# Sums of the FFN weights made in DRAM by accumulating GpSimd transfers, and eleven gated pairs by seven products

## The chip, the core and the metric

One core of a Trainium2 chip runs the whole program. The metric is the device time of one execution in microseconds; lower is better. The engines are TensorE (PE, matmuls), VectorE (DVE), ScalarE (ACT), GpSimd (POOL) and SyncE (SP, which here only issues transfers). Each engine works through its own instructions in a fixed order and waits on semaphores for the others.

## The reference, cut

One hybrid decoder layer over 16 meta tokens and 512 positions (528 columns), model width 1024, in float32:

```
u    = rmsnorm(h);  proj = u @ w_in                       # 52 column blocks of 128
a    = hgrn2(q, f, i, g)                                  # 8 heads, gated linear recurrence
b    = mamba2(z, xbc, dt)                                 # 16 heads, conv + SSD scan
h    = h + concat(a, b) @ w_out
n    = rmsnorm(h);  u = conv3(n @ w_up)                   # w_up: 1024 x 5632
gate, val = split(u)                                      # 22 blocks of 128 each
h    = h + (silu(gate) * val) @ w_down
y    = rmsnorm(h)[:, 16:]
```

## The kernel before

Features lie on the 128 partitions and tokens on the free axis. Every float32 weight tile (128x1024, 512 KB, called a chunk) is split into two `fp32r` parts, `hi` (an ACT copy) and `lo` (a DVE subtraction of `hi` from the raw tile), and every product is made of three matmuls: hi·hi, hi·lo and lo·hi. The list `chunks` holds all chunks in the order of use. `ahead` loads and splits two chunks further than the one in use; the tags `raw`, `whi` and `wlo` have three buffers each, so a chunk's raw load waits until the split three chunks earlier has been done, and its split waits until the matmuls three chunks earlier have been done. A list scheduler lays down each engine's order when the program is built, from priorities (weights are preferred by 100000, evacuations of PSUM by 150000).

The stages, in order of time: Mamba-2, then the eight HGRN heads (`hgrn_head`, three weight chunks each), `hgrn_norm` after heads 3 and 7, the eight gate products, the output projection, the FFN's up-projection, and the down-projection. `hgrn_norm` writes the inverse norms to DRAM (`rs_d`), reads each back spread over the partitions (`rb`) and multiplies each head's output `o` by it in place.

The up-projection works on 22 pairs of a gate block j and a value block 22+j. `KINDS` gives each pair a kind. U and N pairs are direct: two chunks, 96 matmuls of 258 or 256 columns (U uses tokens that are not yet normalised and scales the result). A W pair (`scheme`) halves the contraction and the tokens, in the manner of Strassen and Winograd, and makes seven half-size products instead of eight: 84 matmuls of 258 columns. Its weights come as three chunks from `scheme_weights`: `w0` is the gate block itself, `w2` holds the sums s1 and s2, and `w1` holds two further tiles plus a fourth sum s4 in buffers of the tag `ab`. Before, the two raw blocks are loaded (two transfers), and DVE makes four sums of 128x512 in SBUF. After the seven products, one ACT copy and six DVE additions (lines 965 to 971) put the results together out of PSUM, and `taps` applies the three-tap convolution.

`STEPS` and `SPLITS` hang other work on the pairs' ends: normalising the tokens, and splitting finished activations `ac` for the down-projection. POOL does a few memsets early on and four multiplications at the very end; it issues no transfer.

Of the kernel before, what the change touches and what calls it, by code (L numbers as in the profile page):

```python
# [7 lines left out]
F32 = mybir.dt.float32  # L8
# [3 lines left out]
ALU = mybir.AluOpType  # L12
# [3 lines left out]
P = 128  # L16
# [3 lines left out]
T0 = META - 2  # L20
NB = 4
DM = 1024
KD = DM // P
FF = 2816
KF = FF // P
# [22 lines left out]

KINDS = "UUUUUUUUNWNWWNWNWWNWWN"
STEPS = {0: (0, 1), 1: (2,), 2: (3,), 3: (4,), 4: (5,), 5: (6,), 6: (7,)}
SPLITS = {7: (0,), 8: (1, 2), 10: (3,), 13: (4,), 15: (5,), 18: (6,), 20: (7, 8), 21: range(9, 22)}
HT = 258
NUNSC = 5

# [4 lines left out]
def tile_block(ctx: ExitStack, tc: tile.TileContext, xT, w_in, w_dt, w_out, w_up, w_down,  # L61
               par, consts, consti, out, dbg=None):
    nc = tc.nc
    V, A, G, PE = nc.vector, nc.scalar, nc.gpsimd, nc.tensor

    cp = ctx.enter_context(tc.tile_pool(name="cp", bufs=1))
# [5 lines left out]
    dp = ctx.enter_context(tc.tile_pool(name="dp", bufs=1, space=DRAM))  # L72

    def slot(name, n=NT, dtype=F32, parts=P, tag="m"):
        return gp.tile([parts, n], dtype, tag=tag, name=name, bufs=TAGS[tag])

    def first(offset=100000):
        return tc.high_priority(offset=offset)
# [31 lines left out]
    V.memset(eps, EPS)  # L110
    LOGS = "natural_log_exp_and_others"
    warm = cp.tile([P, 1], F32, name="warm")
    with first(300000):
        w = A.activation(warm[:], eps[:], AF.Copy)
        with tc.issue_after(w.ins):
            A.preload_act_table_set(LOGS)
# [30 lines left out]
    chunks = [(("in", j), w_in[j], KD) for j in order]  # L147
# [3 lines left out]
    chunks += [(("out", j, s), w_out[j][:, s * KD * P:(s + 1) * KD * P], KD) for j, s in oorder]  # L151
    for j in range(KF):
        if KINDS[j] == "W":
            chunks += [(("w0", j), w_up[j], KD), (("w2", j), w_up[KF + j], KD), (("w1", j), None, KD)]
        else:
            chunks += [(("up", j), w_up[j], KD), (("up", KF + j), w_up[KF + j], KD)]
    def dn(j, k0, kc):
# [5 lines left out]
    wdone = {}  # L163
    wnext = [0]

    def raw_tile(key):
        return wp.tile([P, KD * P], F32, tag="raw", name="raw_" + "_".join(map(str, key)), bufs=3)

    def split_tiles(key):
        name = "_".join(map(str, key))  # L170
        return (wp.tile([P, KD * P], F32R, tag="whi", name=f"whi_{name}"),
                wp.tile([P, KD * P], F32R, tag="wlo", name=f"wlo_{name}"))
# [4 lines left out]
    def split_weights(raw, hi, lo, d, eng):  # L177
        A.activation(hi[:, d], raw[:, d], AF.Copy)  # L178
        eng.tensor_tensor(lo[:, d], raw[:, d], hi[:, d].bitcast(F32), ALU.subtract)  # L179

    HK = KD * P // 2
    sums = {}

    def split_half(x, hi, lo):
        A.activation(hi, x, AF.Copy)
        V.tensor_tensor(lo, x, hi.bitcast(F32), ALU.subtract)

    def scheme_weights(key, src):


        kind, j = key
        if kind == "w0":
            sums[j] = [raw_tile(key)]
            nc.sync.dma_start(sums[j][0][:], src)
            hi, lo = split_tiles(key)
            split_weights(sums[j][0], hi, lo, slice(0, 2 * HK), V)
            return hi, lo
        if kind == "w2":
            rg, rv = sums[j][0], raw_tile(key)
            nc.sync.dma_start(rv[:], src)  # L200
            s1, s2 = slot(f"s1_{j}", 512, tag="ab"), slot(f"s2_{j}", 512, tag="ab")
            V.tensor_tensor(s1[:], rv[:, 0:HK], rv[:, HK:], ALU.add)
            V.tensor_tensor(s2[:], s1[:], rg[:, 0:HK], ALU.add)
            sums[j] += [rv, s2]
            hi, lo = split_tiles(key)
            split_half(s1[:], hi[:, 0:HK], lo[:, 0:HK])
            split_half(s2[:], hi[:, HK:], lo[:, HK:])
            return hi, lo
        rg, rv, s2 = sums.pop(j)
        V.tensor_tensor(rv[:, 0:HK], rv[:, 0:HK], rg[:, 0:HK], ALU.add)  # L210
        V.tensor_tensor(rg[:, HK:], rg[:, HK:], s2[:], ALU.add)
        hi, lo = split_tiles(key)
        split_weights(rv, hi, lo, slice(0, 2 * HK), V)
        h4, l4 = slot(f"s4h_{j}", 512, F32R, tag="ab"), slot(f"s4l_{j}", 512, F32R, tag="ab")
        split_half(rg[:, HK:], h4[:], l4[:])
        return hi, lo, h4, l4

    def ahead(n):
        while wnext[0] < min(n, len(chunks)):
            key, src, kc = chunks[wnext[0]]  # L220
            if key[0] in ("w0", "w1", "w2"):
                with first():
                    wdone[key] = scheme_weights(key, src)
                wnext[0] += 1
                continue
            with first():
                raw, hi, lo = raw_tiles(key)
                d = slice(0, kc * P)
                nc.sync.dma_start(raw[:, d], src)
                split_weights(raw, hi, lo, d, V)  # L230
            wdone[key] = (hi, lo)
            wnext[0] += 1
# [24 lines left out]
    with first(200000):  # L257
        for k in range(0, KD, 2):
            d = slice(k * P, (k + 2) * P)
            for j, w, kx in ((BT, starts[0], k), (CT, starts[1], k + 1)):  # L260
                t = slot(f"x{kx}", tag="y")
# [8 lines left out]
        for k in range(KD):  # L270
# [3 lines left out]
            tag = "b0" if k < 4 else "b1"  # L274
            hi, lo = slot(f"v{k}_hi", dtype=F32R, tag=tag), slot(f"v{k}_lo", dtype=F32R, tag=tag)
# [23 lines left out]
    with first():  # L299
        for n, (a0, a1) in enumerate(((0, HALF), (HALF, NT))):  # L300
            p = bank(f"psn{n}")
# [49 lines left out]
    for n, (a0, a1) in enumerate(((0, HALF), (HALF, NT))):  # L351
        p = bank(f"psd{n}")[0:66, :]
# [305 lines left out]
    os_ = []  # L658
# [138 lines left out]

    for h in range(NH):
        hgrn_head(h)
        if h % 4 == 3:  # L800
            hgrn_norm(h - 3)
    oah, oal = [], []
    for h in range(NH):
# [6 lines left out]
        hi, lo = slot(f"oa{h}_hi", dtype=F32R), slot(f"oa{h}_lo", dtype=F32R)  # L810
# [10 lines left out]
    for j, s in oorder:  # L821
        w = weights("out", j, s)
# [10 lines left out]
        hi, lo = slot(f"u2h{j}", dtype=F32R, tag="u"), slot(f"u2l{j}", dtype=F32R, tag="u")  # L833
# [92 lines left out]
    def scheme(j):  # L926

        p1, p2, p6 = (bank(f"p{n}_{j}")[:, 0:HT] for n in (1, 2, 6))
        p75, p43 = banks2(f"p75_{j}"), banks2(f"p43_{j}")
        H = KD // 2  # L930
        b11 = [(nh[k][:, tails[0]], nl[k][:, tails[0]]) for k in range(H)]
        b21 = [(nh[k][:, tails[0]], nl[k][:, tails[0]]) for k in range(H, KD)]
        b22 = [(nh[k][:, tails[1]], nl[k][:, tails[1]]) for k in range(H, KD)]
        t1, t2, t3, t4 = ([t[n] for t in ts] for n in range(4))

        def mul(ps, hi, lo, xs):
            for k, (xh, xl) in enumerate(xs):
                wh, wl = hi[:, k * P:(k + 1) * P], lo[:, k * P:(k + 1) * P]
                PE.matmul(ps, wh, xh, start=k == 0, stop=False)  # L939
                PE.matmul(ps, wh, xl, start=False, stop=False)  # L940
                PE.matmul(ps, wl, xh, start=False, stop=k == H - 1)  # L941


        sg, sv, su = (slot(f"s{n}{j}", 2 * HT, tag=t) for n, t in (("g", "L"), ("v", "L"), ("u", "pr")))
        cs = [slot(f"fc{i}", 512, tag="pr") for i in (j, KF + j)]
        A_, B_ = slice(0, HT), slice(HT, 2 * HT)

        def two(ps):
            return ps[:].rearrange("p (a t) -> p a t", a=2)[:, :, 0:HT]

        def by_halves(t):
            return t[:].rearrange("p (a t) -> p a t", a=2)

        hi, lo = weights("w0", j)
        mul(p1, hi[:, 0:HK], lo[:, 0:HK], b11)
        mul(p2, hi[:, HK:], lo[:, HK:], b21)
        hi, lo = weights("w2", j)
        mul(p6, hi[:, HK:], lo[:, HK:], t2)
        mul(p75[:, 512:512 + HT], hi[:, 0:HK], lo[:, 0:HK], t1)
        hi, lo, h4, l4 = weights("w1", j)  # L960
        mul(p75[:, 0:HT], hi[:, 0:HK], lo[:, 0:HK], t3)
        mul(p43[:, 512:512 + HT], h4, l4, b22)
        mul(p43[:, 0:HT], hi[:, HK:], lo[:, HK:], t4)
        with evac():
            A.activation(sg[:, A_], p1, AF.Copy)
            V.tensor_tensor(sv[:, A_], sg[:, A_], p6, ALU.add)
            V.tensor_tensor(sg[:, A_], sg[:, A_], p2, ALU.add)
            V.tensor_tensor(by_halves(su), sv[:, A_].unsqueeze(1).broadcast_to([P, 2, HT]), two(p75), ALU.add)
            V.tensor_tensor(sv[:, B_], su[:, A_], p75[:, 512:512 + HT], ALU.add)
            V.tensor_tensor(sv[:, A_], su[:, A_], p43[:, 0:HT], ALU.add)  # L970
            V.tensor_tensor(sg[:, B_], su[:, B_], p43[:, 512:512 + HT], ALU.add)
        for c, r, i in ((cs[0], sg, j), (cs[1], sv, KF + j)):
            w = taps_of(j) if r is sg else [ntap[:, n * KF + j:n * KF + j + 1] for n in range(3)]
            taps(by_halves(c), by_halves(r), i, w, col(C_FB + i))
        return cs
# [157 lines left out]
```

## Time and profile before

| | us |
|---|---|
| median of 3 runs | 882.2 (881.79 to 883.04) |
| profiled execution, first to last instruction (span) | 880.9 |
| PE busy in it | 861.5 |
| DVE busy | 596.4 |
| ACT busy | 438.7 |
| POOL busy | 8.9 |

The profile gives its execution's own time only as the span, 880.9 us; what lies around the span is not in it, and the median of the runs is 1.3 us above the span. "Busy" counts the union of an engine's instructions; a matmul is pipelined, so one of 258 columns is shown with some 282 ns although the next begins after 120 ns. In a table by stretches, "busy (x n)" is the busy time and the number of instructions in the stretch. In a timeline, the brackets hold the idle time before an instruction and what ended it.

### The profile page before, as it was taken

Reading aid. Unit: us, or ns where it says so; the run is one execution under the profiler, and the core shown is the slowest. Engines: PE = TensorE matmul, PEld = TensorE weight load, DVE = VectorE, ACT = ScalarE, POOL = GpSimd, SP = SyncE. Lnnn points to the kernel's source line nnn. Section 1 sums busy time; section 2 is a strip of 40 time slices with the busy share of each in tenths; the row PEclk is TensorE's granted clock in tenths of the full one; section 3 lists DMA queues with packets and bytes.
Section 4 is the critical chain, followed back from the end, with each engine's and each line's share of the span. In section 5 each row is a group of like instructions: output and inputs, shape, how many; then the busy total and the mean of one; then the engine's idle time right before and its main releaser. Section 6 shows DMA issues by size and latency. Waiting matters only on the chain.

```text
span 880.9 us, 16283 instructions
## 1 busy us (share of the span) xinstructions
PE 861.5 (98%) x6840; PEld 821.5 (93%) x6840; DVE 596.4 (68%) x1012; ACT 438.7 (50%) x688; POOL 8.9 (1%) x30
## 2 busy tenths in 40 slices
PE   7999999999999999999999999999999999999995
PEld 6999898999999999999999999999999999888885
DVE  6984977788776766444334469888999997633333
ACT  7638985966446444363222265445455555433221
POOL 1000000000000000000000000000000000000001
PEclk9999999999999999999999999999999999999998
DMA  7234242212221222245233223322133314243312
GB/s 247 91 114 154 88 133 72 73 53 69 73 62 60 100 70 72 85 137 163 97 96 97 89 81 96 97 96 90 56 117 100 120 56 131 66 110 105 90 43 95
DMA packets 29081, 84.64 MB, mean 96 GB/s; under 512 B 3128, under 2 KB 6712, under 8 KB 29008
## 3 DMA queue, kind: packets, MB, share of 16 engines
q1 hardware_dynamic: 26480, 80.02, 29.2%
q10 hardware_dynamic: 2528, 3.60, 1.4%
q8 instruction: 53, 0.87, 0.4%
q14 instruction: 20, 0.16, 0.1%
HBM read 81.45 MB, written 2.15 MB: 95 GB/s over the span
## 4 chain that ended last, share of the span: by engine, by line
PE 96%; ACT 1%; DMA 1%; DVE 1%; issue 1%; DVEq 0%; SPq 0%; ACTq 0%
PE pj L250 33%; PE pup L250 18%; PE pout L250 10%; PE pdn L1006 3%; PE pdn L1007 3%; PE pdn L1005 3%; PE p L939 3%; PE p L940 3%; PE p L941 3%; PE pdn L1019 1%; PE pdn L1021 1%; PE pdn L1020 1%; PE psy L550 1%; DMA x<-in_xT_dram 1%; PE psy L553 1%; PE pa L752 1%
## 5 line engine op out<-in xcount | busy, mean ns | idle before, releaser
L250 PE MATMUL pj<-u_lo,whi_in 128*128 128x272 f32 (+1 forms) x752 | 157.1, 288 | 0.0
L250 PE MATMUL pj<-u_hi,wlo_in 128*128 128x272 f32 (+1 forms) x752 | 156.3, 286 | 0.0
L250 PE MATMUL pj<-u_hi,whi_in 128*128 128x272 f32 (+1 forms) x752 | 155.3, 287 | 0.0
L250 PEld LDWEIGHTS pj<-u_lo,whi_in 128*128 128x128 f32 x752 | 116.2, 188 | 2.4 <-issue 1.9
L250 PEld LDWEIGHTS pj<-u_hi,wlo_in 128*128 128x128 f32 x752 | 116.6, 189 | 2.0 <-issue 1.9
L250 PEld LDWEIGHTS pj<-u_hi,whi_in 128*128 128x128 f32 x752 | 115.6, 188 | 2.4 <-issue 2.3
L179 DVE TENSOR_TENSOR wlo_in<-raw_in,whi_in 128x1024 fp32r<-128x1024 f32 (+1 forms) x58 | 64.3, 1108 | 55.6 <-ACT whi_in L178 55.4
L178 ACT ACTIVATE whi_in<-raw_in 128x1024 fp32r<-128x1024 f32 (+1 forms) x58 | 56.0, 966 | 64.0 <-PE pj L250 59.1
L179 DVE TENSOR_TENSOR wlo_dn<-raw_dn,whi_dn 128x1024 fp32r<-128x1024 f32 (+1 forms) x24 | 27.3, 1136 | 54.6 <-ACT whi_dn L178 54.6
L178 ACT ACTIVATE whi_dn<-raw_dn 128x1024 fp32r<-128x1024 f32 (+1 forms) x24 | 23.6, 987 | 73.8 <-PE pdn L1006 53.4
L1006 PE MATMUL pdn<-ac_lo,whi_dn 128*128 128x512 f32 (+1 forms) x154 | 55.9, 363 | 0.0
L1005 PE MATMUL pdn<-ac_hi,whi_dn 128*128 128x512 f32 (+1 forms) x154 | 55.6, 361 | 0.0
L1007 PE MATMUL pdn<-ac_hi,wlo_dn 128*128 128x512 f32 (+1 forms) x154 | 55.6, 361 | 0.0
L178 ACT ACTIVATE whi_up<-raw_up 128x1024 fp32r<-128x1024 f32 x28 | 29.7, 1060 | 46.8 <-PE pup L250 23.9
L250 PE MATMUL pup<-u2h,wlo_up 128*128 128x258 f32 (+1 forms) x256 | 51.6, 283 | 0.0
L250 PE MATMUL pup<-u2l,whi_up 128*128 128x258 f32 (+1 forms) x256 | 51.1, 281 | 0.0
L250 PE MATMUL pup<-u2h,whi_up 128*128 128x258 f32 (+1 forms) x256 | 51.1, 282 | 0.0
L178 ACT ACTIVATE whi_out<-raw_out 128x1024 fp32r<-128x1024 f32 x16 | 17.0, 1061 | 55.7 <-PE pout L250 29.9
L179 DVE TENSOR_TENSOR wlo_up<-raw_up,whi_up 128x1024 fp32r<-128x1024 f32 x28 | 34.2, 1220 | 9.8 <-ACT whi_up L178 9.7
L179 DVE TENSOR_TENSOR wlo_out<-raw_out,whi_out 128x1024 fp32r<-128x1024 f32 x16 | 19.6, 1225 | 30.1 <-ACT whi_out L178 30.1
L250 PEld LDWEIGHTS pup<-u2h,wlo_up 128*128 128x128 f32 x256 | 39.3, 188 | 0.1
L250 PEld LDWEIGHTS pup<-u2l,whi_up 128*128 128x128 f32 x256 | 39.3, 189 | 0.0
(357 smaller groups left out, 2186.4 us busy)
## 6 DMA issues: line engine op xcount, KB each, us to landing
raw_in<-in_w_in_dram SPq DMA_DIRECT2D x50, 512.0 KB, 3.6
raw_up<-in_w_up_dram SPq DMA_DIRECT2D x28, 512.0 KB, 3.6
raw_out<-in_w_out_dram SPq DMA_DIRECT2D x16, 512.0 KB, 3.6
raw_w<-in_w_up_dram SPq DMA_DIRECT2D x16, 512.0 KB, 3.7
raw_dn<-in_w_down_dram SPq DMA_DIRECT2D x16, 512.0 KB, 3.9
ab<-acum_d SPq DMA_DIRECT2D x16, 264.0 KB, 4.2
raw_dn<-in_w_down_dram SPq DMA_DIRECT2D x8, 384.0 KB, 3.1
rb<-rs_d SPq DMA_DIRECT2D x8, 257.0 KB, 4.3
```

The source lines that it names most:

```text
L178: A.activation(hi[:, d], raw[:, d], AF.Copy)
L179: eng.tensor_tensor(lo[:, d], raw[:, d], hi[:, d].bitcast(F32), ALU.subtract)
L250: PE.matmul(ps[:, O + a0:O + a1], w, x[:, a0:a1], start=s, stop=e)
L550: PE.matmul(psy[q0:q0 + 64, a0 - META:a1 - META], xdt[b][:, hc], Ls[h][:, a0:a1], start=True, stop=False)
L553: PE.matmul(psy[q0:q0 + 64, a0 - META:a1 - META], ss[b - 1][:, hc], abs_[h][:, a0:a1], start=False, stop=True)
L752: PE.matmul(pa[:, c:c + P], kA[:, META + c:META + c + P], qA[:, c:c + P], start=True, stop=True)
L939: PE.matmul(ps, wh, xh, start=k == 0, stop=False)
L940: PE.matmul(ps, wh, xl, start=False, stop=False)
L941: PE.matmul(ps, wl, xh, start=False, stop=k == H - 1)
L1005: PE.matmul(ps, wh, xh, start=k0 + k == 0, stop=False)
L1006: PE.matmul(ps, wh, xl, start=False, stop=False)
L1007: PE.matmul(ps, wl, xh, start=False, stop=k0 + k == KF - 1)
```

## The change

Eleven pairs instead of eight are of kind W; N pairs go from six to three. The four weight sums of a W pair are no longer made by DVE. Instead, `weight_sums` makes them in a DRAM tile `sums{j}` of four 128x512 slots by six GpSimd transfers per pair: two plain copies (512 KB each) lay down the first halves of the gate and the value block in slots 0 and 1 and the whole gate block in slots 2 and 3; then come accumulating transfers of 512, 256, 256 and 256 KB, each of which adds a further half block, or slot 0 itself, to slots already there. `scheme_weights` then loads ready sums: `w2` in one transfer, `w1` in three.

```
-KINDS = "UUUUUUUUNWNWWNWNWWNWWN"
+KINDS = "UUUUUUUUNWWWWNWWWWWWWN"
+WS = [j for j in range(KF) if KINDS[j] == "W"]
...
+    def weight_sums(js, behind):
+        gate = G.tensor_copy(tick[:], behind)
...
+        with tc.issue_after(gate.ins):
+            for j in js:
+                G.dma_start(ds[j][:, 0:2], halves[j][:, :, 0:HK])
+                G.dma_start(ds[j][:, 2:4], w_up[j].rearrange("p (n c) -> p n c", n=2))
+            for j in js:
+                G.dma_start(ds[j][:, 0:2], twice(w_up[KF + j][:, HK:]), accum_op=ALU.add)
+                G.dma_start(ds[j][:, 2], w_up[KF + j][:, 0:HK], accum_op=ALU.add)
+            for j in js:
+                G.dma_start(ds[j][:, 0], w_up[KF + j][:, 0:HK], accum_op=ALU.add)
+            for j in js:
+                G.dma_start(ds[j][:, 3], ds[j][:, 0], accum_op=ALU.add)
...
+        elif kind == "w2":
+            nc.sync.dma_start(raw[:], sumd[j][:, 0:2 * HK])
+        else:
+            s4 = slot(f"s4_{j}", 512, tag="ab")
+            nc.sync.dma_start(raw[:, 0:HK], sumd[j][:, 2 * HK:3 * HK])
+            nc.sync.dma_start(raw[:, HK:], w_up[KF + j][:, HK:])
+            nc.sync.dma_start(s4[:], sumd[j][:, 3 * HK:])
+        split_weights(raw, hi, lo, slice(0, 2 * HK), V)
...
-            V.tensor_tensor(s1[:], rv[:, 0:HK], rv[:, HK:], ALU.add)
-            V.tensor_tensor(s2[:], s1[:], rg[:, 0:HK], ALU.add)
...
-        V.tensor_tensor(rv[:, 0:HK], rv[:, 0:HK], rg[:, 0:HK], ALU.add)
-        V.tensor_tensor(rg[:, HK:], rg[:, HK:], s2[:], ALU.add)
...
     for h in range(NH):
         hgrn_head(h)
+        if h < len(WS) // 2 + len(WS) % 2:
+            weight_sums(WS[2 * h:2 * h + 2], os_[h][:, T0:T0 + 1])
```

The sums of two pairs hang on each of heads 0 to 5 (one pair on head 5): a POOL copy of one column of the head's output `o` into `tick` stands ahead of that head's twelve transfers. So POOL's queue now reads the `o` tiles that `hgrn_norm` later overwrites.

POOL, in the HGRN heads: before, nothing stands there. Now the queue between the copies into `tick` for heads 2 and 3 holds twelve transfers, of which the last eight and the copy for head 3 read as follows (`sums14` and `sums15` are the DRAM tiles of pairs 14 and 15, `o3` the output of head 3).

```order
L208 DMA sums14_3049<-in_w_up_dram 128x2x512
L209 DMA sums14_3049<-in_w_up_dram 128x512
L208 DMA sums15_3050<-in_w_up_dram 128x2x512
L209 DMA sums15_3050<-in_w_up_dram 128x512
L211 DMA sums14_3049<-in_w_up_dram 128x512
L211 DMA sums15_3050<-in_w_up_dram 128x512
L213 DMA sums14_3049<-sums14_3049 128x512
L213 DMA sums15_3050<-sums15_3050 128x512
L192 COPY tick_81<-o3_3326 128x1
```

The copy for head 3 stands behind all transfers of pairs 14 and 15, and each of these rows waits in the queue until the transfer it adds to has landed: L208 and L209 for the plain copies, L211 for L208, L213 for L211.

DVE, first norm of the HGRN heads (after head 3): before, the four in-place products on `o0` to `o3` stand together, ahead of work of head 4 (`mt0`, `S4`, `sc0`).

```order
L796 SCALAR_TENSOR_TENSOR o0_2482<-o0_2482,pt_75,rb0_3306 128x514
L796 SCALAR_TENSOR_TENSOR o1_2748<-o1_2748,pt_75,rb1_3310 128x514
L796 SCALAR_TENSOR_TENSOR o2_3014<-o2_3014,pt_75,rb2_3314 128x514
L796 SCALAR_TENSOR_TENSOR o3_3280<-o3_3280,pt_75,rb3_3318 128x514
L179 TENSOR_TENSOR wlo_in_14_3647<-raw_in_14_3645,whi_in_14_3646 128x1024
L757 COPY_PREDICATED mt0_2194<-maskA_77,pm4_3529 16x2
L666 TENSOR_SCALAR f5_3642<-f5_3642,lbt_480 128x528
L744 SCALAR_TENSOR_TENSOR S4_3545<-S4_3545,d128_4_3513,pS4_3544 128x128
```

Now:

```order
L814 SCALAR_TENSOR_TENSOR o0_2483<-o0_2483,pt_75,rb0_3367 128x514
L814 SCALAR_TENSOR_TENSOR o1_2764<-o1_2764,pt_75,rb1_3371 128x514
L181 TENSOR_TENSOR wlo_in_14_3723<-raw_in_14_3721,whi_in_14_3722 128x1024
L814 SCALAR_TENSOR_TENSOR o2_3045<-o2_3045,pt_75,rb2_3375 128x514
L775 COPY_PREDICATED mt0_2195<-maskA_77,pm4_3590 16x2
L684 TENSOR_SCALAR f5_3718<-f5_3718,lbt_481 128x528
L762 SCALAR_TENSOR_TENSOR S4_3606<-S4_3606,d128_4_3574,pS4_3605 128x128
L814 SCALAR_TENSOR_TENSOR o3_3326<-o3_3326,pt_75,rb3_3379 128x514
L777 COPY_PREDICATED sc0_2193<-maskA_77,pa4_3615 128x512
```

The product on `o3` moved behind the `mt0` copy and ahead of the `sc0` copy. Each of the products on `o0` to `o5` now also waits for POOL's copy out of that `o`.

PE, end of a run of W pairs before an N pair: before, pair 17 ended (`p43_17`), then four matmuls of the next W pair, 19, stood ahead of the N pair 18 (`pup18`); the same stood between pairs 9 and 10, and two matmuls of the down-projection between pairs 20 and 21.

```order
L941 MATMUL p43_17_8210<-t4_3_6874,wlo_w1_17_8219 128x258
L939 MATMUL p1_19_8469<-n0_hi_6009,whi_w0_19_8340 128x258
L940 MATMUL p1_19_8469<-n0_lo_6010,whi_w0_19_8340 128x258
L939 MATMUL p2_19_8470<-n4_hi_6015,whi_w0_19_8340 128x258
L940 MATMUL p2_19_8470<-n4_lo_6016,whi_w0_19_8340 128x258
L250 MATMUL pup18_8344<-n0_hi_6009,whi_up_18_8251 128x258
```

Now such a place stands between pairs 12 and 13:

```order
L961 MATMUL p43_12_7632<-t4_3_6958,wlo_w1_12_7640 128x258
L959 MATMUL p1_14_7888<-n0_hi_6093,whi_w0_14_7764 128x258
L960 MATMUL p1_14_7888<-n0_lo_6094,whi_w0_14_7764 128x258
L959 MATMUL p2_14_7889<-n4_hi_6099,whi_w0_14_7764 128x258
L960 MATMUL p2_14_7889<-n4_lo_6100,whi_w0_14_7764 128x258
L268 MATMUL pup13_7769<-n0_hi_6093,whi_up_13_7676 128x258
```

The two matmuls of the down-projection between pairs 20 and 21 stand as before; inside the runs 9 to 12 and 14 to 20 the W pairs follow each other directly.

More of the change, by code (lines that the diff above doesn't have):

```diff
@@ L112, in tile_block @@
     warm = cp.tile([P, 1], F32, name="warm")
+    tick = cp.tile([P, 1], F32, name="tick")
     with first(300000):
@@ L153, in tile_block @@
         if KINDS[j] == "W":
-            chunks += [(("w0", j), w_up[j], KD), (("w2", j), w_up[KF + j], KD), (("w1", j), None, KD)]
+            chunks += [((w, j), None, KD) for w in ("w0", "w2", "w1")]
         else:
@@ L181, in tile_block @@
     HK = KD * P // 2
-    sums = {}
+    sumd = {}
     def split_half(x, hi, lo):
@@ L186, in split_half, with twice @@
         V.tensor_tensor(lo, x, hi.bitcast(F32), ALU.subtract)
-    def scheme_weights(key, src):
+    def weight_sums(js, behind):
+        gate = G.tensor_copy(tick[:], behind)
+        halves = w_up.rearrange("(a j) p c -> j p a c", a=2)
+        ds = {}
+        for j in js:
+            t = dp.tile([P, 4 * HK], F32, name=f"sums{j}")
+            sumd[j] = t
+            ds[j] = t[:].rearrange("p (n c) -> p n c", n=4)
+        def twice(ap):
+            return ap.unsqueeze(1).broadcast_to([P, 2, HK])
+        with tc.issue_after(gate.ins):
[7 more added lines that the diff above has]
+                G.dma_start(ds[j][:, 0], w_up[KF + j][:, 0:HK], accum_op=ALU.add)
+            for j in js:
+                G.dma_start(ds[j][:, 3], ds[j][:, 0], accum_op=ALU.add)
@@ L191, in scheme_weights @@
+    def scheme_weights(key):
         kind, j = key
+        raw = raw_tile(key)
+        hi, lo = split_tiles(key)
         if kind == "w0":
[L193 to L196, printed above, removed]
-            return hi, lo
[L198 to L202, printed above, removed]
-            V.tensor_tensor(s2[:], s1[:], rg[:, 0:HK], ALU.add)
[L204 to L208, printed above, removed]
@@ L209, in scheme_weights @@
-        rg, rv, s2 = sums.pop(j)
-        V.tensor_tensor(rv[:, 0:HK], rv[:, 0:HK], rg[:, 0:HK], ALU.add)
-        V.tensor_tensor(rg[:, HK:], rg[:, HK:], s2[:], ALU.add)
-        hi, lo = split_tiles(key)
-        split_weights(rv, hi, lo, slice(0, 2 * HK), V)
+            nc.sync.dma_start(raw[:], w_up[j])
+        elif kind == "w2":
[5 more added lines that the diff above has]
+            nc.sync.dma_start(s4[:], sumd[j][:, 3 * HK:])
@@ L214, in scheme_weights @@
+        split_weights(raw, hi, lo, slice(0, 2 * HK), V)
+        if kind != "w1":
+            return hi, lo
         h4, l4 = slot(f"s4h_{j}", 512, F32R, tag="ab"), slot(f"s4l_{j}", 512, F32R, tag="ab")
-        split_half(rg[:, HK:], h4[:], l4[:])
+        split_half(s4[:], h4[:], l4[:])
         return hi, lo, h4, l4
@@ L222, in ahead @@
                 with first():
-                    wdone[key] = scheme_weights(key, src)
+                    wdone[key] = scheme_weights(key)
                 wnext[0] += 1
@@ L957, in scheme @@
         hi, lo = weights("w2", j)
-        mul(p6, hi[:, HK:], lo[:, HK:], t2)
-        mul(p75[:, 512:512 + HT], hi[:, 0:HK], lo[:, 0:HK], t1)
+        mul(p6, hi[:, 0:HK], lo[:, 0:HK], t2)
+        mul(p75[:, 512:512 + HT], hi[:, HK:], lo[:, HK:], t1)
         hi, lo, h4, l4 = weights("w1", j)
```

## Prediction

> **What bounds the kernel now.** I read the page's busy shares and chain first, then the time of each up-projection pair, then the waits there, and last the HGRN stretch, where the new work is put.
>
> ```profile
> PE 861.5 (98%) x6840; PEld 821.5 (93%) x6840; DVE 596.4 (68%) x1012; ACT 438.7 (50%) x688; POOL 8.9 (1%) x30
> PE 96%; ACT 1%; DMA 1%; DVE 1%; issue 1%; DVEq 0%; SPq 0%; ACTq 0%
> 593.95:605.37 11.42, 11.42 (x98) 11.42 (x97) 9.62 (x15) 7.04 (x12) 0.00 (x0) 1.00 0.19 59
> 659.90:670.13 10.23, 10.23 (x86) 10.09 (x85) 8.69 (x13) 5.21 (x8) 0.00 (x0) 1.00 0.54 158
> 605.37:747.96 142.59, 139.41 (x1156) 138.47 (x1155) 128.58 (x197) 74.06 (x103) 0.00 (x0) 1.00 0.33 100
> ```
>
> TensorE is busy 98% and carries 96% of the chain, so time comes off only where matmuls go or PE stops waiting. The three stretches are one N pair (11.42 us for its 96 matmuls; the counts take in neighbours at the edges), one W pair (10.23 us for 84), and all of pairs 9 to 21. In that last stretch VectorE is busy 128.58 of 142.59 us, so it stands close behind PE. PE's clock is granted in full (1.00) throughout.
>
> PE is idle 142.59 − 139.41 = 3.2 us there. The waits are these:
>
> ```profile
> L939 PE MATMUL p<-n_hi,whi_w 128*128 128x258 f32 x64 | 18.1, 284 | 2.1 <-ACT whi_w L178 2.1
> L1019 PE MATMUL pdn<-ac_hi,whi_dn 128*128 128x512 f32 x1 | 0.5, 496 | 1.1 <-ACT whi_dn L178 1.1
> 701.66 0.28 PE L941 MATMUL p<-t,wlo_w 128*128 128x258 f32 x1
> 703.02 0.38 PE L939 MATMUL p<-n_hi,whi_w 128*128 128x258 f32 x1 [1.08 <-ACT whi_w L178]
> 615.52 1.06 ACT L178 ACTIVATE whi_w<-raw_w 128x1024 fp32r<-128x1024 f32 x1 [3.20 <-PE p L940]
> ```
>
> They are the places where matmuls of a later product stand ahead of an N pair. That product's `whi` buffer is the one that the W pair just ending still reads, so ACT can split only then (615.52, released by PE), and PE loses 703.02 − 701.66 − 0.12 = 1.24 us. Three such places: 3.7 us.
>
> **The change, part by part.**
>
> *Three pairs turn from N to W.* Each exchange takes 11.42 − 10.23 = 1.2 us of PE: −3.7 us for three. All of it is on the path.
>
> *The early matmuls.* After the change two of the three places are left (before pair 13, and the down-projection's two before pair 21): −1.2 us.
>
> *VectorE per W pair.*
>
> ```profile
> L179 DVE TENSOR_TENSOR wlo_w<-raw_w,whi_w 128x1024 fp32r<-128x1024 f32 x15 | 18.3, 1221 | 6.2 <-ACT whi_w L178 5.8
> L902 DVE SCALAR_TENSOR_TENSOR fc<-sg,pt,fc 128x512 f32<-128x512 f32 x16 | 11.9, 744 | 0.9 <-ACT fc L900 0.9
> L186 DVE TENSOR_TENSOR wlo_w<-s,whi_w 128x512 fp32r<-128x512 f32 x14 | 9.0, 682 | 1.0 <-ACT whi_w L185 1.0
> L202 DVE TENSOR_TENSOR s<-raw_w 128x512 f32<-128x512 f32 x7 | 4.8, 687 | 2.2 <-DMA raw_w<-in_w_up_dram 2.2
> L211 DVE TENSOR_TENSOR raw_w<-raw_w,s 128x512 f32<-128x512 f32 x7 | 4.8, 683 | 0.0
> L988 DVE TENSOR_TENSOR ac<-fc,fc 128x512 f32<-128x512 f32 x13 | 8.9, 683 | 0.1
> L968 DVE TENSOR_TENSOR su<-sv,p 128x516 f32<-128x516 f32 x8 | 5.5, 681 | 0.0
> L970 DVE TENSOR_TENSOR sv<-su,p 128x258 f32<-128x258 f32 x8 | 3.3, 416 | 0.5 <-PE p L941 0.5
> L179 DVE TENSOR_TENSOR wlo_up<-raw_up,whi_up 128x1024 fp32r<-128x1024 f32 x10 | 12.2, 1218 | 0.7 <-ACT whi_up L178 0.6
> L902 DVE SCALAR_TENSOR_TENSOR fc<-pup,pt,fc 128x512 f32<-128x512 f32 x20 | 14.9, 747 | 0.3
> ```
>
> Before, a W pair costs DVE two splits of 1.22, three half splits of 0.68 (L186: two in `w2`, one for s4), four sums of 0.69 (L202, L211 and two like them), four taps of 0.74, one addition of 0.68 (L968), five of 0.42 (L970 and its neighbours), and the gate at 0.68 (L988): 13.7 us, against 10.2 on PE. After, the sums go and the two half splits of `w2` become one of 1.22: 10.8 us. An N pair costs 2 × 1.22 + 4 × 0.75 + 0.68 = 6.1 us. So W pairs still cost DVE 0.6 us more than PE, and they now come in runs of four and seven. The run of seven, with four activation splits of 0.68 hung into it, puts DVE 7 × 0.6 + 2.7 = 6.9 us behind; the run of four 2.4 + 0.7 = 3.1 us. Bounds for what PE waits there: nothing, because a run of two W pairs before (2 × 3.5 = 7.0 us behind) shows no wait but those above; or all 10 us, if runs this long find no slack. I take 1.0 us, near the lower bound: the row of before is the same lag. If the cover goes, the late thing is the `lo` half of `w1`.
>
> *Weight loads of a W pair* grow from two transfers (1.05 MB) to five (512 + 512 + 256 + 256 + 256 KB, 1.84 MB). The W stretch above moved 158 GB/s × 10.23 us = 1.6 MB with no wait, and a raw buffer comes round once per pair, every 10.2 us.
>
> ```profile
> raw_in<-in_w_in_dram SPq DMA_DIRECT2D x50, 512.0 KB, 3.6
> raw_w<-in_w_up_dram SPq DMA_DIRECT2D x16, 512.0 KB, 3.7
> rb<-rs_d SPq DMA_DIRECT2D x8, 257.0 KB, 4.3
> q1 hardware_dynamic: 26480, 80.02, 29.2%
> POOL ot L1063 <- ACT rs L1054: 696.3, 2, 691.2
> ```
>
> A load lands in 3.7 us, and the split of 1.06 + 1.22 follows: 6 us of 10.2. Cost nothing, by that cover.
>
> *The sums.* POOL is idle for 691 us in one piece, so its 66 transfers take no work from it. They cost only through others: who waits for POOL's queue, and who shares the DMA engines. All this lies in the HGRN heads:
>
> ```profile
> 208.47 0.17 ACT L772 ACTIVATE o<-pm 128x2 f32<-128x2 f32 x1
> 289.72 0.76 DVE L796 SCALAR_TENSOR_TENSOR o<-o,pt,rb 128x514 f32<-128x514 f32 x1 [2.12 <-DMA rb<-rs_d]
> 295.40 0.75 DVE L796 SCALAR_TENSOR_TENSOR o<-o,pt,rb 128x514 f32<-128x514 f32 x1 [2.00 <-DMA rb<-rs_d]
> 297.21 0.14 DVE L757 COPY_PREDICATED mt<-maskA,pm 16x2 f32<-16x2 int32 x1
> 297.27 0.54 DVE L666 TENSOR_SCALAR f<-f,lbt 128x528 f32<-128x528 f32 x1
> 297.40 0.38 PE L770 MATMUL pm<-mt 128*128 128x2 f32 x2 [0.84 <-DVE mt L757]
> 200.00:400.00 200.00, 199.16 (x1737) 193.00 (x1737) 131.13 (x292) 94.97 (x141) 0.00 (x0) 1.00 0.27 82
> ```
>
> The norm's product on `o3` overwrites what POOL's copy for head 3 reads, so it now waits for that copy, which stands behind the 36 transfers of heads 0 to 2. These can start at 208.6, when head 0's column is written, and the product starts at 295.40: 86.8 us, or 28.9 us per group of twelve. No row shows an accumulating transfer. Per group, the low end is four dependent steps at the landing time of 3.7 us with everything else beneath them, 15 us; the high end is all twelve one behind the other, 44 us. The group has two independent pairs and its copies need no wait, so I take 24 us, nearer the low end: 14 us to spare, cost nothing.
>
> The DMA engines: q1 moved 80.02 MB in 29.2% of 16 × 880.9 us, 51 engine-us per MB. A pair's sums write 2.36 MB, of which 1.31 MB are added and so also read from the target: for six pairs 14.2 to 22 MB, 45 to 70 us of all sixteen engines, in 86.8 us where 27% (23 us) are taken already. It fits, at the upper end only just. What it delays first is `rb`, which DVE already waits for (2.12 and 2.00 us); between 0 and one more landing, 4.3 us. I take 1.0. Against it stands the 0.84 us that PE lost behind the `o3` product: the copy for `mt` now stands ahead of it, −0.8.
>
> **Sum.** −3.7 − 1.2 + 1.0 + 1.0 − 0.8 = −3.7 us: the span goes from 880.9 to 877.2 us. The median stands 1.3 us above the span, so I forecast 882.2 − 3.7 = 878.5 us.
>
> **The rivals.**
>
> *A. POOL comes late (slower).* Decides at the product on `o3`. If a group takes G us, DVE stops for 3G − 86.8 there, and everything behind it (the `sc` copy, head 5's chain, the weight splits) stops PE. The four dependent steps of each group speak for it, and DMA engines up to (70 + 23)/86.8 = 107% taken; POOL's empty queue and the two pairs in parallel speak against. From G = 30.5 on it eats the whole gain. At G = 33, 12.2 us late: 882.2 − 4.7 + 12.2 = 889.7 us, where 4.7 is the gain without the 1.0 for `rb`. At the high end, G = 44: 923 us.
>
> By the Trainium skill (DMA: Bandwidth & Descriptors, "Anatomy of one DMA — SWDGE (gpsimd) path") such a transfer takes about 2.0 us plus its bytes at 436 GB/s; as an estimate from that, a pair's six one behind the other are 17.4 us, six pairs 104 us, 18 us late, which would give 895 us. No run here shows it yet; whether it applies hangs on how far the two pairs overlap. A second rule of the skill (SBUF — State Buffer, "Who interferes with whom") lets a VectorE instruction that takes both port pairs lock GpSimd out while it writes descriptors; the `f` row above, 0.54 us, is of that sort, and twelve such per group would add 6.5 us to G and make 24 us into 30.5, where the gain is gone. That is this same rival, reached by another way.
>
> *B. VectorE bounds the runs of W pairs.* Half to all of the 10 us instead of 1.0: +4 to +9, so 882.5 to 887.5 us. For it: 10.8 against 10.2 us per pair. Against: 7.0 us behind was hidden before.
>
> *C. Full gain.* No PE wait in the W runs and `rb` on time: −5.7, 876.5 us.
>
> *D. The transfers hold up others but not POOL:* `rb` a landing late, 4.3 instead of 1.0: 881.8 us, no measurable change.
>
> **How the numbers follow.** The forecast with its near variants 0.44 (own range 876.5 to 881), C 0.09, A 0.28, B 0.10, D 0.09. A change below 0.2% (1.8 us) can hardly be told here, as the three runs spread over 1.25 us; "same" therefore reaches from 880.4 to 884.0. Faster: the forecast less 0.03 at its upper edge, C, and 0.04 of A (late by under 3 us), 0.54. Same: that 0.03, D, 0.04 of A and 0.04 of B, 0.20. Slower: the rest of A (0.20) and of B (0.06), 0.26. The range goes from 875 (a little beyond C) to 893 us, which takes in A up to G = 34; above it lie some 0.13, below 0.04.
>
> **What would show it.** Right: the stretch of pairs 9 to 21 takes about 139 us, PE's waits there are two of 1.1 us and little else; DVE's product on `o3` waits for `rb` and not POOL; POOL's twelve transfers stand within 23 to 29 us. Wrong: a DVE wait on POOL's copy in the product on `o2` or `o3` with PE idle behind it (A); PE waiting for `wlo_w` in pairs 16 to 20 (B); `raw_in` landing much later than 3.6 us with ACT's splits waiting for it.

## The result and the profile after

| | before | after |
|---|---|---|
| median, four runs each | 882.5 us | 904.5 us (900.9 to 909.0) |
| ratio | 1 | 1.025 (95% interval 1.022 to 1.028) |
| span of the profiled execution | 880.9 us | 903.4 us |

The change makes the kernel 2.5% slower, where 0.4% faster was forecast. Two slow executions (906.0 us of number 4 below, 1054.4 us of before beside numbers 5 to 8) are left out of all medians. The page of after, in the order busy shares, slices of the span (PE, its clock, DMA), the new queue, the chain:

```profile
PE 862.5 (95%) x6804; PEld 822.4 (91%) x6804; DVE 588.2 (65%) x996; ACT 444.2 (49%) x689; POOL 66.7 (7%) x102
PE   7999999999999469998999999999999999999995
PEclk9999999999999779999999999999999999999998
DMA  7334332126788888888532232334464654233312
q0 software_dynamic: 10912, 25.96, 15.4%
PE 80%; issue 8%; DMA 5%; POOL 3%; DVE 2%; ACT 2%; SPq 0%; DVEq 0%; ACTq 0%; POOLq 0%
```

PE is as busy as before but has a hole in slices 14 and 15 (a slice is 22.6 us, so about 294 to 339 us), and its clock falls there too. It lies in the HGRN heads, where the DMA engines went from 27% to about 80%. The chain, before 96% PE, now has 16% of issue, DMA and POOL; the largest part is POOL's queue, through which it runs for 112 us (from 208.71 to 321.13). The waits name the place (columns: total, times, longest):

```profile
PE po L786 <- DVE sc L781: 13.8, 1, 13.8
PE pm L788 <- DVE mt L775: 6.1, 1, 6.1
PE pj L268 <- ACT sg L828: 3.2, 2, 2.5
DVE o L814 <- POOL tick L192: 16.3, 1, 16.3
DVE o L814 <- DMA rb<-rs_d: 20.9, 5, 10.5
POOL sums L208 <- issue: 50.4, 9, 7.7
```

In the timeline, DVE's products of the first norm (L814) and what PE waited for:

```profile
298.09 0.75 DVE L814 SCALAR_TENSOR_TENSOR o<-o,pt,rb 128x514 f32<-128x514 f32 x1 [10.50 <-DMA rb<-rs_d]
303.97 0.14 DVE L775 COPY_PREDICATED mt<-maskA,pm 16x2 f32<-16x2 int32 x1
304.17 0.59 PE L788 MATMUL pm<-mt 128*128 128x2 f32 x2 [6.08 <-DVE mt L775]
321.15 0.76 DVE L814 SCALAR_TENSOR_TENSOR o<-o,pt,rb 128x514 f32<-128x514 f32 x1 [16.32 <-POOL tick L192]
323.85 0.29 DVE L781 COPY sc<-pb 32x128 f32<-32x128 f32 x1
324.29 0.77 PE L786 MATMUL po<-sc,vt 128*128 128x128 f32 x2 [13.81 <-DVE sc L781]
```

Two delays follow each other. DVE waits 10.50 us for `rb` of head 0 (2.12 before), and the `mt` copy queued behind it stops PE for 6.08 us. Then the product on `o3` waits 16.32 us for POOL's copy of a column of `o3`, and the `sc` copy behind it stops PE for 13.81. POOL's queue shows why that copy is late (its three copies behind heads 1 to 3, and the accumulating transfers of head 1's group between the first two):

```profile
244.96 0.49 POOL L192 COPY tick<-o 128x1 f32<-128x1 f32 x1
257.14 1.18 POOL L208 DMA_DIRECT2D sums<-in_w_up_dram  x1 [1.68 <-issue]
268.30 1.18 POOL L208 DMA_DIRECT2D sums<-in_w_up_dram  x1 [6.20 <-issue]
277.11 1.69 POOL L211 DMA_DIRECT2D sums<-in_w_up_dram  x2 [6.19 <-issue]
284.09 0.66 POOL L192 COPY tick<-o 128x1 f32<-128x1 f32 x1
320.63 0.49 POOL L192 COPY tick<-o 128x1 f32<-128x1 f32 x1
```

Head 0's copy stood at 208.71, so three groups took 111.9 us, 37.3 each. Some 70% of a group are stops, among them those before the second 512 KB accumulate (L208), for which the profile names no releaser ("issue"). The third part of the loss is the clock (columns: busy and number for PE, PEld, DVE, ACT, POOL, then PE's clock, DMA share, GB/s); the last row is pairs 9 to 21:

```profile
302.30:309.20 6.90, 5.04 (x23) 5.04 (x24) 2.25 (x5) 0.17 (x1) 2.02 (x2) 0.51 0.96 174
312.60:329.60 17.00, 5.31 (x24) 5.34 (x25) 8.36 (x23) 1.23 (x2) 5.93 (x9) 0.50 0.76 155
633.29:770.37 137.08, 134.92 (x1120) 134.29 (x1119) 121.78 (x185) 79.35 (x104) 0.00 (x0) 1.00 0.53 157
```

PE's 5.04 + 5.31 us of work in the first two stretches ran at half clock, which loses about 5 us. The account of the span's +22.5 us, by the times at which PE starts the same product in both traces: +23.1 up to head 4's products with `sc` (13.8 + 6.1 of waits less the old 0.84, and 4.0 of clock), +0.9 in head 5, +3.7 at the second norm (its `rb` is late too), and −5.5 in pairs 9 to 21. The rest is unchanged within 0.3. This is PE's time in order, not a list of separate causes: the products with `sc` start when POOL's copy lets DVE go on, so up to there the late `rb` and the half clock only take the place of a longer wait.

### The profile page after: what moved, and what is told of

The parts are those of the page before. It is cut to its first block, busy times and chain, and to the rows that moved or that the text cites. A ratio compares the mean times of both kernels' runs of the same rounds, so it can differ in the third digit from the quotient of the medians.

```text
span 903.4 us, 16410 instructions
## 1 busy us (share of the span) xinstructions
PE 862.5 (95%) x6804; PEld 822.4 (91%) x6804; DVE 588.2 (65%) x996; ACT 444.2 (49%) x689; POOL 66.7 (7%) x102
## 4 chain that ended last, share of the span: by engine, by line
PE 80%; issue 8%; DMA 5%; POOL 3%; DVE 2%; ACT 2%; SPq 0%; DVEq 0%; ACTq 0%; POOLq 0%
PE pj L268 22%; PE pup L268 14%; PE pout L268 10%; PE p L960 4%; PE p L959 4%; PE p L961 4%; PE pdn L1026 3%; PE pdn L1027 3%; PE pdn L1025 3%; DMA sums<-in_w_up_dram 2%; DMA rb<-rs_d 2%; PE pdn L1039 1%; PE pdn L1041 1%; PE pdn L1040 1%; PE psy L568 1%
## 5 line engine op out<-in xcount | busy, mean ns | idle before, releaser
L180 ACT ACTIVATE whi_dn<-raw_dn 128x1024 fp32r<-128x1024 f32 (+1 forms) x24 | 23.6, 988 | 73.2 <-PE pdn L1026 53.4
L960 PE MATMUL p<-t,whi_w 128*128 128x258 f32 x176 | 50.0, 284 | 0.0
L959 PE MATMUL p<-t,whi_w 128*128 128x258 f32 x176 | 49.8, 283 | 0.0
L961 PE MATMUL p<-t,wlo_w 128*128 128x258 f32 x176 | 49.6, 282 | 0.0
L180 ACT ACTIVATE whi_w<-raw_w 128x1024 fp32r<-128x1024 f32 x33 | 35.0, 1060 | 28.6 <-PE p L960 16.1
L181 DVE TENSOR_TENSOR wlo_w<-raw_w,whi_w 128x1024 fp32r<-128x1024 f32 x33 | 40.3, 1221 | 11.8 <-ACT whi_w L180 11.7
L180 ACT ACTIVATE whi_up<-raw_up 128x1024 fp32r<-128x1024 f32 x22 | 23.3, 1060 | 43.0 <-PE pup L268 23.9
```

## The experiments

Before runs at 882.3 us beside the first four kernels, 882.6 beside the next four, 882.9 beside the last three. Theories in the expectations: Q is POOL's ordered queue, whose copy holds up DVE; T is the traffic of the sums; R the room for descriptors; B the bytes and the accumulating itself. Where only a start-to-start time is given, it is read as in the account above.

**1. POOL gates on a private copy.** ACT copies the column, so nobody waits for POOL.

```
-            weight_sums(WS[2 * h:2 * h + 2], os_[h][:, T0:T0 + 1])
+            mine = cp.tile([P, 1], F32, name=f"mine{h}")
+            A.activation(mine[:], os_[h][:, T0:T0 + 1], AF.Copy)
+            weight_sums(WS[2 * h:2 * h + 2], mine[:])
```

> The changed kernel, except that ACT first copies the gate column of each head's output into a tile of its own, and POOL's gate reads that tile; so the norm's product on o3 no longer waits for POOL's queue. Same transfers, same heads. Theory Q (POOL's queue, through the overwritten o tile, stops DVE): DVE's 16.3 us wait on POOL's copy and PE's 13.8 us wait for the sc copy go, PE's clock no longer falls there for long; the late rb loads (PE 6.1 us) and the second norm (3.2 us) stay: 886 to 889 us. Theory T (the traffic itself holds everything up, the queue is incidental): the wait comes back under another name, within 3 us of the changed kernel's 904.5.

Measured 889.1 us (888.0 to 892.4), ratio 1.008 (1.006 to 1.010): 15.5 us of the loss are gone. Its waits:

```profile
PE pm L788 <- DVE mt L775: 3.8, 1, 3.8
DVE o L814 <- DMA rb<-rs_d: 21.8, 6, 8.7
```

The groups are as slow as before (POOL's copies of heads 2 and 3 at 281.19 and 320.13), only nobody waits. So Q is the larger part. What remains, 10.9 us of the profiled span before the FFN's gain of 5.5, is the late `rb` at both norms: PE waits of 3.8 and 2.7 us and two stretches at half clock behind them.

**2. The sums in the output projection**, two pairs behind each of its first products instead of behind the heads.

```
-            weight_sums(WS[2 * h:2 * h + 2], os_[h][:, T0:T0 + 1])
...
+        if j < len(WS) // 2 + len(WS) % 2:
+            weight_sums(WS[2 * j:2 * j + 2], xr[:, T0:T0 + 1])
```

> The changed kernel with the same transfers hung on the output projection's results xr0 to xr5 instead of on heads 0 to 5; nothing overwrites an xr tile before the end. Theory Q: the HGRN heads run as before the change, the up-projection keeps its gain of 5.4 us (stretch from pair 9 to pair 21: 137 us against 142.5), so 876 to 878 us against 882.5. Theory T: the same traffic now makes raw_out, xr and later raw_up land late, and PE waits there by some 10 us: 885 us or more.

Measured 881.8 us, ratio 0.998 (0.997 to 1.000), between the numbers of the two theories, but in two groups: four runs at 877.3 to 878.6, eight at 881.7 to 883.8. The profiled one, of the lower group, has the heads as in before and the output projection undelayed, as Q expects. The upper group is taken up in number 11.

**3. More descriptor room**, 1984 instead of 1024 bytes per partition; order and gates as in after.

```
-    ... dynamic_dma_scratch_size=1024)
+    ... dynamic_dma_scratch_size=1984)
```

> The changed kernel with 1984 bytes per partition instead of 1024 for the GpSimd descriptors (all that is free); every engine's order is the same. Theory R (POOL's stop of 8 us ahead of the second L208 of each group is for room for descriptors): that stop goes, a group takes under 31 us instead of 36.5, the wait on o3 falls from 16.3 us to under 3, time 886 to 892 us. Theory B (the DMA engines' rate for accumulating transfers sets the group's time): the second L208 starts earlier but lands no earlier, a group still takes 34 to 37 us, time 900 to 905 us.

Measured 884.2 us (881.3 to 885.6), ratio 1.002 (1.000 to 1.003).

```profile
266.29 0.48 POOL L192 COPY tick<-o 128x1 f32<-128x1 f32 x1
300.59 0.50 POOL L192 COPY tick<-o 128x1 f32<-128x1 f32 x1
DVE o L814 <- DMA rb<-rs_d: 15.2, 6, 7.5
```

From head 0's copy (208.29) to head 3's 92.3 us pass, 30.8 per group: the stop before the second accumulate is gone, which makes 6.5 us per group. Head 3's copy now comes in time (the product on `o3`, late by `rb`, stands at 302.42), so no DVE product waits for POOL any more; again `rb` remains. That one number of the launch recovers 20 of the 22 us. R is shown, and a little better than expected.

**4. Plain copies in place of the accumulates**, same sizes and order. The additions are left out.

```
-                G.dma_start(ds[j][:, 2], w_up[KF + j][:, 0:HK], accum_op=ALU.add)
+                G.dma_start(ds[j][:, 2], w_up[KF + j][:, 0:HK])
```

(and so in all four)

> The changed kernel with the four accumulating transfers of each pair as plain copies of the same slices (it leaves out the additions). Same order, same waits, same count of transfers; only the read of the target goes. Theory B: L208 to L213 land in some 5 us instead of 8 to 9, a group takes 22 to 27 us, the wait on o3 goes, time 882 to 888 us. If the steps' fixed latency sets the group's time instead: landings of 7 us and more, groups of 32 us and more, 893 us or more.

Measured 882.7 us, ratio 1.000 (0.999 to 1.001).

```profile
255.01 1.28 POOL L192 COPY tick<-o 128x1 f32<-128x1 f32 x1
279.26 1.20 POOL L192 COPY tick<-o 128x1 f32<-128x1 f32 x1
```

Three groups take 70.7 us (from 208.59 on), 23.6 each: what the prediction put down for a group is right for copies. Accumulating costs 13.7 us per group more with the small room. Number 3 takes 6.5 of these away without touching the additions, so R and B each hold for about half, if the two add up.

**5. All sums behind the second norm**, room 1920 bytes.

```
+    mine = cp.tile([P, 1], F32, name="mine")
+    A.activation(mine[:], os_[7][:, T0:T0 + 1], AF.Copy)
+    for n in range(0, len(WS), 2):
+        weight_sums(WS[n:n + 2], mine[:])
```

> The changed kernel with all sums behind the second norm of the HGRN heads: POOL's gates read one column that ACT copied from o7 after that norm, and the descriptors have 1920 bytes per partition. Theory Q with R (the loss is POOL's queue and the traffic beside the two norms, nothing else): the heads run as before, the sums take from some 393 to 570 us, well before pair 9, the up-projection keeps 5.4 us: 876 to 878 us, in one cluster. Theory T (the same traffic costs wherever it is put): waits of PE in the output projection or in pairs 0 to 7, 881 us or more, as in most executions with the sums hung on the output projection.

Measured 882.2 us (881.7 to 882.9), ratio 0.999 (0.998 to 1.000): the number of theory T. The heads are undisturbed and pairs 9 to 21 take 137.1 us, but the output projection takes 97.6 instead of 91.1:

```profile
458.65 0.80 PE L268 MATMUL pout<-ob_hi,whi_out 128*128 128x258 f32 x2 [3.01 <-ACT whi_out L180]
456.40 0.72 ACT L856 ACTIVATE u2h<-xr,pt 128x514 fp32r<-128x514 f32 x1 [9.19 <-DVE xr L852]
457.56 2.94 ACT L180 ACTIVATE whi_out<-raw_out 128x1024 fp32r<-128x1024 f32 x3
458.50:465.30 6.80, 6.62 (x29) 6.33 (x30) 3.52 (x4) 1.99 (x3) 1.32 (x3) 0.50 0.97 145
409.90:507.49 97.59, 94.55 (x771) 94.05 (x770) 34.03 (x38) 25.68 (x32) 33.93 (x41) 0.97 1.04 273
```

PE waits 3.01 us for a weight split, and the 6.8 us after run at half clock, which loses another 3.4: together the 6.5 us. With no pacing, the sums also fill the DMA engines (share 1.04 over the whole output projection). But T's mechanism is not what the trace shows. The split is late because ACT's order has `u2h`, which needs the result `xr` of the product just running, ahead of it: ACT stands idle for 9.19 us, and the split follows. Its load had been issued at 431.4, 26 us earlier, and no load of this weight with a known landing took more than 10.7. In before, after and number 9 the split stands ahead of `u2h`. So the list scheduler laid ACT's order differently in this program, and the 6.5 us come from that order; why it did so, and what the traffic alone would cost, stays open.

**6. Eleven pairs with the old sums on DVE** (the new `KINDS` in the old kernel).

> The kernel before, with eleven W pairs in the changed order but the sums made by DVE as before: one part of the change alone. By the sums of the prediction DVE has 13.7 us per W pair against 10.2 on PE; the run of seven puts it 24.5 + 2.7 us behind, of which some 10 us can be hidden: PE waits for some 14 to 20 us, time 890 to 898 us. Rival (DVE's lag is hidden in long runs too): no such waits, 877 to 879 us, and then the transfers were not needed for the eleven pairs.

Measured 891.7 us (891.3 to 892.3), ratio 1.010 (1.008 to 1.011).

```profile
605.16:757.06 151.90, 138.80 (x1120) 135.22 (x1118) 144.48 (x234) 79.99 (x115) 0.00 (x0) 1.00 0.31 93
PE p L939 <- ACT whi_w L185: 4.2, 3, 1.6
PE p L941 <- DVE s4l L186: 2.9, 2, 1.6
```

DVE is busy 144.48 of 151.90 us and PE waits for splits, as the first expectation has it. Eleven pairs need the sums off DVE.

**7. The old eight pairs with the new sums**, placed as in number 5.

> As the run before last, with the old eight W pairs in the old order: the other part alone. If all of the gain comes from the three exchanged pairs and the place of the early matmuls: the stretch from pair 9 to 21 stays at 142 to 142.6 us and the time at 881.5 to 882.5 us. If the relief of DVE (2.7 us for each W pair) is worth something to PE: 879 to 880 us.

Measured 880.4 us (880.1 to 880.5), ratio 0.997 (0.996 to 0.998).

```profile
604.81:744.70 139.89, 138.69 (x1153) 137.98 (x1152) 112.00 (x161) 72.87 (x95) 0.00 (x0) 1.00 0.45 137
PE pup L268 <- DVE sv L991: 1.2, 4, 0.3
```

DVE falls from 128.58 to 112.00 us there, and the stretch by 2.7 us though no product is saved; the time is just above the second expectation's range. But PE's order changed too: the matmuls of a later product, which stood ahead of an N pair at three places of before and cost 1.24 us each, stand there no more, and PE waits only four times 0.3 us for `sv`. That makes 3.7 − 1.2 = 2.5 of the 2.7 us. So this run does not show that a relieved DVE is worth something by itself.

**8. Twelve pairs**, 9 to 20, placed as in number 5.

```
-KINDS = "UUUUUUUUNWWWWNWWWWWWWN"
+KINDS = "UUUUUUUUNWWWWWWWWWWWWN"
```

> As the first of these four, with twelve W pairs in one run from 9 to 20 (pair 13 too). One more exchange (1.2 us) and one place of early matmuls less (1.2 us): 2.4 us under the first of these four if DVE's 10.8 us per W pair against PE's 10.2 still hides, that is 874 to 876 us; PE waits for wlo_w late in the run, and 877 us or more, if DVE falls too far behind (12 times 0.6 us and five activation splits, 10.6 us).

Measured 879.7 us (879.1 to 880.2), ratio 0.996 (0.995 to 0.998). The step from eleven, 2.4 us, is as expected; the level is missed by the same wait of 3.0 us for `whi_out`, with ACT's order as in number 5, and by a stretch of 3.4 us at half clock behind it.

**9. The sums spread out:** one pair at a time, behind heads 0, 1, 2, 4, 5 and 6 on private copies, none beside the first norm, the other five behind the output projection's products; room 1728 bytes.

```
+        if h in (0, 1, 2, 4, 5, 6):
+            mine = cp.tile([P, 1], F32, name=f"mine{h}")
+            A.activation(mine[:], os_[h][:, T0:T0 + 1], AF.Copy)
+            n = h - h // 4
+            weight_sums(WS[n:n + 1], mine[:])
...
+        n = 6 + j
+        if n < len(WS):
+            weight_sums(WS[n:n + 1], xr[:, T0:T0 + 1])
```

> The sums of one pair at a time, eleven times: behind heads 0, 1, 2, 4, 5 and 6 (on private copies of the gate column, none behind head 3, so that nothing runs beside the first norm) and behind the output projection's products 0 to 4; descriptor room 1728 bytes. Theory S (bunched traffic is what delays the loads and the rb rows; a pair alone every 12 to 24 us does not): no PE wait above 1.1 us before the feed-forward part, heads and output projection as before, pairs 9 to 21 in 137 us, 876 to 878 us. Theory T (the amount of traffic beside the loads decides, however it is spread): a PE wait of 2 to 4 us behind rb or behind whi_out, followed by a stretch at half clock, 881 to 884 us.

Measured 876.8 us (876.4 to 877.0), ratio 0.993 (0.992 to 0.995), inside what theory S gave.

```profile
604.51:741.62 137.11, 134.95 (x1119) 134.38 (x1118) 121.78 (x185) 79.36 (x104) 0.00 (x0) 1.00 0.52 157
PE pm L788 <- DVE mt L775: 0.2, 1, 0.2
DVE o L814 <- DMA rb<-rs_d: 6.6, 6, 2.2
208.70 1.89 POOL L192 COPY tick<-mine 128x1 f32<-128x1 f32 x1 [33.15 <-ACT mine L820]
232.27 0.81 POOL L192 COPY tick<-mine 128x1 f32<-128x1 f32 x1
411.00:502.00 91.00, 91.00 (x770) 91.00 (x769) 34.55 (x39) 25.90 (x33) 21.22 (x30) 1.00 0.84 195
```

`rb` is as early as in before, the full gain of pairs 9 to 21 is there, and the output projection, at a DMA share of 0.84, takes its 91 us. The amount of traffic did not change, so theory T falls: what counts is when the transfers run. This run changes several things at once, though. One pair runs at a time, POOL reads private copies, the room is larger, and POOL issues nothing beside either norm (none between 279.8 and 297.5, nor between 369.3 and 427.9). That `rb` is late in after and in numbers 1, 3 and 4, where transfers run beside the norm, and on time in numbers 2, 5 and 9, where none do, speaks for the place; that spreading alone would do is not shown. One pair alone takes 232.27 − 208.70 = 23.6 us.

**10. The same with twelve pairs.**

> The same with twelve pairs by seven products (9 to 20) and the twelfth pair's sums behind product 5 of the output projection. Theory S: 874 to 876 us, about 2.4 below the eleven, the difference that the two had with all sums behind the second norm. Theory T: 879 to 881 us.

Measured 875.9 us (874.5 to 876.1), ratio 0.992 (0.990 to 0.994), the fastest kernel here. The step from eleven is only 0.9 us: in the profiled run a stretch at half clock stands at the end of the pairs.

```profile
729.10:732.60 3.50, 3.50 (x10) 2.72 (x10) 3.22 (x5) 2.02 (x3) 0.00 (x0) 0.51 0.45 143
PE pdn L1045 <- ACT whi_dn L180: 1.1, 1, 1.1
PE pdn L1047 <- DVE wlo_dn L181: 0.5, 1, 0.5
```

**11. Number 2 once more,** for a profile of its upper group.

> The kernel with the sums in the output projection (two pairs behind each of its products 0 to 5, descriptor room 1024) once more, for its profile: its times fell into two groups, 877.3 to 878.6 and 881.7 to 883.8 us, and the profile shown came from the lower. If this profile is of the upper group, theory T expects in it a PE wait of 2 to 4 us behind a load in the output projection with a stretch at half clock behind it, together 4 us; the other theory (a clock granted lower over the whole run) expects the same waits as in the lower group and every stretch 0.5% longer.

This run took 881.0 us, between the two groups and nearer the upper.

```profile
PE p L959 <- ACT whi_w L180: 2.0, 2, 1.6
PE pup L268 <- DVE sv L989: 1.2, 1, 1.2
PE p L961 <- DVE wlo_w L181: 0.8, 1, 0.8
502.00:594.00 92.00, 91.37 (x765) 91.06 (x765) 78.26 (x120) 50.19 (x74) 25.26 (x30) 1.00 0.94 223
```

Neither expectation held. The lost time is not in the output projection, and the clock is full. It is in W pair 11 and just behind pair 12: the sums still run during the FFN (DMA share 0.94), and PE waits 4.0 us for splits and for the DVE sum `sv`, against 1.6 in the lower profile (1.1 for `whi_w`, 0.5 for `sv`). The chain into these waits begins with a load of `raw_w` that took 9.7 us (4.5 is the median in after), so here late loads do cost PE time. The two spans, 879.2 and 876.8, also differ by 2.4 us, but that the numbers agree is in part chance, since the lower profile loses time at half clock behind its own waits (3.4 us from 648.0 on) and this one does not. Whether every run of the upper group loses its time there stays open.

## Why the prediction was wrong

**The step that failed is the duration of a group of twelve transfers.** It was put at 24 us, "nearer the low end" of 15 to 44, with 14 us to spare and so at no cost. It took 37.3. Number 4 shows that 24 is what copies take; accumulating and the small descriptor room make the rest (numbers 3 and 4). The bounds held it, but the low end was taken from a load's 3.7 us, while these transfers took about 8:

```profile
sums<-in_w_up_dram POOLq DMA_DIRECT2D x33, 512.0 KB, 8.1
sums<-in_w_up_dram POOLq DMA_DIRECT2D x22, 256.0 KB, 7.9
```

The first row mixes two plain copies with one accumulate per pair. Line by line the medians in after are 7.7 and 8.0 us for the copies (L205, L206), then 9.4 (L208), 9.1 (L209), 6.1 (L211) and 6.3 (L213) for the accumulates; as plain copies in number 4 these four took 7.0, 6.3, 4.0 and 4.0. With such a price unknown and 28.9 us allowed per group, about the middle of 15 to 44, the chance of rival A belonged nearer to a half than to 0.28.

**Rival A is what happened,** in the place and by the wait it named. Its own formula with G = 37.3 gives 3 × 37.3 − 86.8 = 25.1 us late and 882.2 − 4.7 + 25.1 = 902.6 us, against 904.5. The lateness is right by mechanism, not by luck: the product on `o3` came 25.8 us later than before (321.15 against 295.40). That the whole agrees within 2 us is in part luck, since PE lost only 23.1 there, and 4.6 more in head 5 and at the second norm, which the formula does not have. By the Trainium skill (DMA: Bandwidth & Descriptors, "Anatomy of one DMA — SWDGE (gpsimd) path") six pairs in series came to 104 us; the three groups measured 111.9, and one pair alone 23.6 where that estimate gave 17.4. This rule of the Trainium skill pointed the right way and was still too low. The lock of the prediction's second rule was not tested.

**The `rb` term, +1.0, was mis-sized.** DVE's first product with `rb` starts 8.4 us later than before (298.09 against 289.72), which costs 6.1 us of PE at the first norm; the same at the second norm costs 3.7, of which the sum has nothing. The bound of "one more landing", 4.3, fails for two reasons. It was taken from rows where the DMA engines were a quarter busy, and it counts one transfer where two follow each other: the store of `rs_d` is issued at 285.3 in both traces, but the load of `rb` behind it at 291.27 instead of 286.56, so 4.7 of the 8.4 us are lost before the load begins. (The profile ties only one `rb` load of after to its landing, 10.5 us; two of before, 3.1 and 5.5.) Number 1 shows that this step alone would have undone the forecast: nobody waits for POOL there, and the kernel still takes 889.1 us, 10.6 above the 878.5. The −0.8 behind it never came, for the same reason; with `rb` on time (number 9) the wait does shrink to 0.2.

**A term was missing:** PE's clock after its waits. The prediction counted a wait at its own length. In after about 5 us of PE's work are lost that way, most of it ahead of products that POOL's copy holds up anyhow; in number 5 a wait of 3.0 us cost 6.5 in all.

**The feed-forward part was right, a little low.** Forecast −3.9, measured −5.5: three pairs −3.6, and the loss beyond the pairs' own matmuls from 142.6 − (8 × 10.23 + 5 × 11.42) = 3.6 us to 137.1 − (11 × 10.23 + 2 × 11.42) = 1.7. Two waits of 1.1 at early matmuls are left, as said. The +1.0 for DVE in the long runs did not occur, so rival B fell. Its premise was a misreading: DVE's instructions overlap in the rows, so their mean durations add up to more than the engine is busy (8 × 13.7 + 5 × 6.1 = 140 us by the prediction's sums, 128.58 in its own row). Scaled by these two numbers, as an estimate, a W pair now costs DVE 9.9 us, less than PE's 10.2, and there is no lag to hide. Rival C's 876.5 us is what number 9 comes to at 876.8, once the transfers are out of the way. The allowance of 86.8 us, and who waits behind it, were read right.

## What to carry to other kernels

A copy on another engine that only times something still reads its source, and whoever overwrites that source waits for everything queued ahead of it; gate on a private copy. When work moves to idle DMA engines, ask which small load on the critical path lands meanwhile, and place the transfers so that no such load meets them: the same bytes cost 22 us behind the heads, gated on `o` and beside the norms, and nothing away from the norms, on private copies and one pair at a time. An edit that moves work also moves the orders that the scheduler lays down; compare the engines' orders in the two traces before a difference is put down to traffic or to a relieved engine (numbers 5 and 7). A price that no row shows should be bounded from the operation's own kind, and with an unknown that close to its allowance the chances should say so.

## What the runs showed of the hardware that was not expected

- Accumulating transfers within DRAM landed in 9.4 us (512 KB, L208) and in 9.1, 6.1 and 6.3 us (256 KB, L209, L211, L213) in after, as plain copies of the same slices in 7.0, 6.3, 4.0 and 4.0 (number 4, medians). A group with accumulates took 37.3 us against 23.6 with copies.
- With 1024 bytes of descriptor room POOL stopped 6 to 8 us before the second of two 512 KB accumulates; with 1984 the group took 6.5 us less.
- PE's clock halved around and after its waits for 3.4, 6.8 or 17 us. After a wait of 3.0 us it cost as much again as the wait (number 5). By the Trainium skill (TensorE: Matmul & The Clock Gate, "What's actually happening") the gate works in windows of 3.4 us, and the lengths here are multiples of that. But the advice of the Trainium skill (the same page, "Why this matters for your kernels") to avoid idle gaps above some 3 us isn't the whole condition: in number 10 the stretch at half clock follows waits of only 1.1 and 0.5 us. The wait of 1.1 at the same place in number 9 is followed by none, nor are the same two waits, 1.1 and 0.5, in number 8; so the lengths of the waits alone do not decide it here.
